# Two low-part tiles moved by 128 bytes, and six small vector loads moved up the load queue, in a decoder trunk on one core

## The chip, the cores and the metric

The kernel runs on one core of a Trainium2 chip. The metric is the device time of one execution in microseconds (us). TensorE (PE) multiplies, and loads the stationary operand of a product in an instruction of its own (PEld); VectorE (DVE) and ScalarE (ACT) work element by element; SyncE (SP) issues all the loads here.

## The reference

Two layers, each of three sublayers on a stream `x` of 256 tokens by 1024 channels in float32:

```python
x = layer_norm(ALPHA * x + 0.5 * swiglu(x, ffn_w1[l, 0], ffn_w2[l, 0]), ...)
x = layer_norm(ALPHA * x + hybrid_mixer(x, w_in[l], ...), ...)
x = layer_norm(ALPHA * x + 0.5 * swiglu(x, ffn_w1[l, 1], ffn_w2[l, 1]), ...)
```

`swiglu` multiplies by 1024x5632 weights, gates (`silu(g) * u`) and multiplies by 2816x1024. `hybrid_mixer` has one 1024x7168 input projection (parts b, c, v, x, y and two merge gates), a short gated convolution, a linear recurrence with 256x256 gate matrices per head, two 1024x1024 output projections (`w_out_conv`, `w_out_rnn`), a gated merge, and a last 1024x1024 projection `w_o`.

## The kernel before

**Split products.** Every operand of a product is split in a high part and a low part (`hi` and `lo` for weights, `xh` and `xl` for the stream, `yh` and `yl` or slots for other activations), and a product is three matmuls: high by high, low activation by high weight, high activation by low weight. `high` (L202) makes the high part of a weight unit on ACT, `low` (L207) the low part on DVE.

**Weight units.** Weights come in units of 1 MB (128 partitions by 2048 floats), numbered in the order of use. SP loads a unit into `raw` (four buffers, L198), then ACT and DVE fill `hi` and `lo` (six buffers each). The main loop emits up to `LOOK` = 6 units ahead of the units that are used up. Units 0 and 1 are loaded in pieces ahead of it, between the loads of `x`.

**Shapes.** In the first part of each sublayer the weights are stationary (128x128) and the stream moves, 256 columns at a time: these are the groups `gu`, `c`, `v`, `b`, `x`, `y`, `ga`, `gb`, `wc`, `wr`, `rg`, all recorded at `mm` (L216). `mm_cols` issues eight products of `xh` by `hi`, eight of `xl` by `hi` and eight of `xh` by `lo`, then takes the next 128 weight columns (`wr` and `rg` in shorter groups). In `form_b` (group `acc`) and in `filler` (group `fill`) it is the other way round: activations are stationary and weights move, 512 columns at a time (256 in a few). `filler` opens each sublayer, while the second half of the tokens is still being normalised; it ends in products of the shape that follows it.

**Addresses.** The tiles of the pool `const` lie one behind the other in the order of their lines, then come the buffers of `raw`, `hi`, `lo` and the activation slots, all of whose sizes are multiples of 4096 bytes in a partition. `xh` and `xl` have 8192 bytes in a partition, `yh` and `yl` (eight rows of 256 floats and a spare of 128 floats) 8704, `gB` and `bB` 4096 each, `vec` 832, `hbm` and `hrg` 128 each, `sp2` and each of the six `sp_` tiles 64; `tiny` and `mhalf` take 32 each. From `xh` to the first weight buffer that makes 43584 = 85 x 512 + 64 bytes. So modulo 512 bytes the weights, and the activation slots, lie 64 past `xh`, and `xl`, `yh` and `yl` lie level with `xh`. `split` (L231) places the hidden rows of `swiglu` 16 floats (64 bytes) into `yh` and `yl`, which puts those level with the weights.

**The opening.** The steps of the first sublayer are `opening` (units 0 and 1, with transposes of `x` among the products), then the products of units 2 and 3 in `fill`, then `gu` from unit 4 on. `load_vectors` issues six small loads into the tile `rows` (L129): biases, convolution taps and recurrence parameters, 104 KB in all. `vectors_pe` turns them on PE (group `vps`, L135), ACT copies the result to `vec`, and `vectors_post` works out a few constants on DVE. They are first used in the mixer. The scheduler keeps each engine's queue in order once it is laid down: PE runs its instructions in program order.

Of the kernel before, what the change touches and what calls it, by code (L numbers as in the profile page):

```python
# [9 lines left out]
F32 = mybir.dt.float32  # L10
# [4 lines left out]
P = 128  # L15
# [25 lines left out]
def trunk_kernel(  # L41
# [21 lines left out]
    _, S, D = x.shape  # L63
    DEPTH = w_in.shape[0]
    DFF = ffn_w2.shape[2]
    NT = S // P
    KD = D // P
# [5 lines left out]
    NPAIR = KD // 2  # L73

    const = ctx.enter_context(tc.tile_pool(name="const", bufs=1))
# [7 lines left out]
    def slot(name, dt=F32):  # L83
        return act.tile([P, 2, S], dt, tag="s", name=name)

    def bank(name):
        return pw.tile([P, 512], F32, tag="w", name=name)

    def f(ap):
        return ap.bitcast(F32)  # L90

    ident = const.tile([P, P], F32, name="ident")
    xtok = const.tile([P, NT, D], F32, name="xtok")
    xh = const.tile([P, KD, S], F32R, name="xh")
    xl = const.tile([P, KD, S], F32R, name="xl")
    yh = const.tile([P, KD * S + 128], F32R, name="yh")
    yl = const.tile([P, KD * S + 128], F32R, name="yl")
    gB = const.tile([P, D], F32, name="gB")
    bB = const.tile([P, D], F32, name="bB")
# [2 lines left out]
    NV = 13 * KD  # L102
    O_BM, O_SC, O_RC, O_RB, O_RG, O_A = 0, 2 * KD, 5 * KD, 9 * KD, 10 * KD, 12 * KD
    vec = const.tile([P, DEPTH, NV], F32, name="vec")
    hbm = const.tile([P, DEPTH, 2 * KD], F32, name="hbm")
    hrg = const.tile([P, DEPTH, 2 * KD], F32, name="hrg")
    sp2 = const.tile([P, DEPTH, KD], F32, name="sp2")
    tiny = const.tile([P, 1], F32, name="tiny")

# [9 lines left out]
    def load_vectors():  # L119
        r = slot("rows")[:NV, :, :P]  # L120
        for src, o, n in (
            (b_merge, O_BM, 2 * KD),
            (sc_w.rearrange("l k d -> l (k d)"), O_SC, 3 * KD),
            (rc_w.rearrange("l k d -> l (k d)"), O_RC, 4 * KD),
            (rc_b, O_RB, KD),
            (rg_b.rearrange("l k d -> l (k d)"), O_RG, 2 * KD),
            (a_param, O_A, KD),
        ):
            nc.sync.dma_start(out=r[o : o + n], in_=src.rearrange("l (r p) -> r l p", p=P))  # L129
        rows.extend(r[:, l, :] for l in range(DEPTH))  # L130
# [7 lines left out]
    def vectors_post():  # L138
        nc.vector.tensor_scalar_mul(hbm, vec[:, :, O_BM : O_BM + 2 * KD], 0.5)
        nc.vector.tensor_scalar_mul(hrg, vec[:, :, O_RG : O_RG + 2 * KD], 0.5)  # L140

        a = vec[:, :, O_A : O_A + KD]
        shp = [P, DEPTH, KD]
        t = {n: const.tile(shp, F32, name=f"sp_{n}") for n in ("na", "e", "base", "d", "q", "acc")}
        nc.vector.scalar_tensor_tensor(t["na"], a, -1.0, a, op0=ALU.mult, op1=ALU.min)
        nc.gpsimd.memset(t["base"], math.e)
        nc.gpsimd.tensor_tensor(t["e"], t["base"], t["na"], op=ALU.pow)
        nc.vector.tensor_scalar_add(t["d"], t["e"], 2.0)
        nc.vector.reciprocal(t["d"], t["d"])
        nc.vector.tensor_mul(t["d"], t["d"], t["e"])  # L150
        nc.vector.tensor_mul(t["q"], t["d"], t["d"])
        nc.vector.tensor_scalar_mul(t["acc"], t["q"], 1.0 / 19)
        for n in (17, 15, 13, 11, 9, 7, 5, 3):
            nc.vector.scalar_tensor_tensor(
                t["acc"], t["acc"], 1.0 / n, t["q"], op0=ALU.add, op1=ALU.mult
            )
        nc.vector.scalar_tensor_tensor(t["acc"], t["acc"], 1.0, t["d"], op0=ALU.add, op1=ALU.mult)
        nc.vector.tensor_scalar(t["na"], a, -1.0, 0.0, op0=ALU.mult, op1=ALU.max)
        nc.vector.scalar_tensor_tensor(
            t["na"], t["acc"], 2.0, t["na"], op0=ALU.mult, op1=ALU.add  # L160
        )
        nc.vector.tensor_scalar_mul(sp2, t["na"], 2.0)


    units = []
# [13 lines left out]
    def unit_half(parts, h):  # L179

        n = 512 // len(parts)
        srcs = []
        for i, (w, c0) in enumerate(parts):
            s = w[h * 512 : (h + 1) * 512, c0 : c0 + n].rearrange("(k p) c -> p k c", p=P)
            srcs.append((i * n, s))
        return unit(srcs, (4, 512))

    def load_unit(u, parts=1):
        u.raw = praw.tile([P, 2048], F32, tag="raw", name="raw")
        u.hi = phi.tile([P, 2048], F32R, tag="hi", name="hi")  # L190
        u.lo = plo.tile([P, 2048], F32R, tag="lo", name="lo")
        view = lambda t: t.rearrange("p (a b) -> p a b", b=u.shape[-1])
        u.h, u.l = view(u.hi), view(u.lo)
        n = u.shape[0] // parts
        for i in range(parts):
            ks = slice(i * n, (i + 1) * n)
            for c0, src in u.srcs:
                u.load = nc.sync.dma_start(out=view(u.raw)[:, ks, c0 : c0 + src.shape[-1]], in_=src[:, ks])  # L198
# [29 lines left out]
    def row(t, k, n, shift=0):  # L228
        return t[:, shift + k * S : shift + (k + n) * S]

    def split(name, v, j=NPAIR, shift=0):  # L231


        if j < NPAIR:
            h, lo = (row(t, 2 * j, 2, shift).rearrange("p (a b) -> p a b", b=S) for t in (yh, yl))
        else:
            h, lo = slot(name + "h", F32R), slot(name + "l", F32R)
        nc.scalar.copy(h, v)
        nc.vector.tensor_sub(lo, v, f(h))
        return h, lo  # L240
# [163 lines left out]
    def ffn(l, i, n, last):  # L404
        w1, w2 = ffn_w1[l, i], ffn_w2[l, i]
        hs = {}
        opens = (l, i) == (0, 0)
        nfill = NFILL if opens else 1
        fill = [unit_half([(w1, 256 * b), (w1, DFF + 256 * b)], h) for b in range(nfill) for h in range(2)]
        ga, up = {}, {}  # L410
        for j in range(nfill, NPF):
            ga[j] = unit_a(w1, 256 * j)
            up[j] = unit_a(w1, DFF + 256 * j)
        us = [unit_b(w2, q) for q in range(NPF)]

        def swish(g, u, shape, name):

            v = slot(name)
            o = v.rearrange("p a b -> p (a b)")[:, : shape]
            nc.scalar.activation(o, g, AF.Tanh, scale=0.5)  # L420
            nc.vector.scalar_tensor_tensor(o, o, 1.0, g, op0=ALU.add, op1=ALU.mult)
            nc.vector.tensor_mul(o, o, u)  # L422
            return v

        tok = {}

        def post_fill(t, b, ps):
            tok[t, b] = swish(ps[:, 0:256], ps[:, 256:512], 256, "hf")

        filler(fill, post_fill, not opens)  # L430

        def fill_transposes(b):
            ps = bank("hT")
            h, lo = slot("h0h", F32R), slot("h0l", F32R)
            for t in range(NT):
                v = tok[t, b].rearrange("p a b -> p (a b)")
                for c in range(2):
                    with tc.issue_after(last_mm[0]):
                        nc.tensor.transpose(
                            ps[:, c * S + t * P : c * S + (t + 1) * P], v[:, c * P : (c + 1) * P], ident  # L440
                        )
            p3 = ps.rearrange("p (c s) -> p c s", s=S)
            nc.scalar.copy(h, p3)
            nc.vector.tensor_sub(lo, p3, f(h))
            hs[b] = h, lo

        banks = {}

        def pe(j, which, u):
            b = bank("gu")  # L450
            banks[j, which] = b
            for c in range(2):
                mm_cols(b[:, c * S : (c + 1) * S], u, c * P, x_pairs())

        def post(j):
            v = swish(banks[j, 0], banks[j, 1], 512, "hv")
            hs[j] = split("h", v, j - 5 if 5 <= j < 9 else NPAIR, 16)

        for j in range(nfill, NPF):
            step(lambda j=j: pe(j, 0, ga[j]), None, 1, [ga[j]])  # L460
            if 1 <= j - nfill <= nfill:
                step(lambda b=j - nfill - 1: fill_transposes(b))
            step(lambda j=j: pe(j, 1, up[j]), lambda j=j: post(j), 1, [up[j]])

        form_b(us, lambda q, kk, t: [v[:, kk, t * P : (t + 1) * P] for v in hs[q]], 0.25, l, n, last)
# [216 lines left out]
    for hh in range(2):  # L682
        load_x(hh)
        load_unit(units[hh], 2)
    done, freed = 2, 0
    for i, (pe, post, free, need) in enumerate(steps):
        while i and done < min(len(units), freed + LOOK):
            emit_unit(units[done])
            done += 1
            if done == 4:  # L690
                load_vectors()
        if pe:
            pe()
        if post:
            post()
        freed += free
        if i == 2:
            vectors_pe()
            vectors_post()
# [29 lines left out]
```

## Time and profile before

| | us |
|---|---|
| three runs | 1213.77, 1220.48, 1223.33 |
| median | 1220.48 |
| the profiled execution | 1221.89 |
| its span | 1220.1 |

PE is busy for 99% of the span (DVE for 67%, ACT for 48%). Products are pipelined, so the time that one takes from start to end is longer than the distance between starts; what counts is the distance, which the chain of waits gives as the length of a piece divided by its count. A row of the chain has the start of the piece in us from the start of the span, its length in us, and what ran. A row of the timeline has start, length (to the modelled end of the last product), engine, line, operation, what it writes and reads, shape and count. A row of the stretches has the bounds, the length, the busy time and count on PE, PEld, DVE, ACT and POOL, the granted TensorE clock, the share of time in which DMA engines were busy, and GB/s.

### The profile page before, as it was taken

Reading aid. Unit: us, or ns where it says so; the run is one execution under the profiler, and the core shown is the slowest. Engines: PE = TensorE matmul, PEld = TensorE weight load, DVE = VectorE, ACT = ScalarE, POOL = GpSimd, SP = SyncE. Lnnn points to the kernel's source line nnn. Section 1 sums busy time; section 2 is a strip of 40 time slices with the busy share of each in tenths; the row PEclk is TensorE's granted clock in tenths of the full one; section 3 lists DMA queues with packets and bytes.
Section 4 is the critical chain, followed back from the end, with each engine's and each line's share of the span. In section 5 each row is a group of like instructions: output and inputs, shape, how many; then the busy total and the mean of one; then the engine's idle time right before and its main releaser. Section 6 shows DMA issues by size and latency. Waiting matters only on the chain.

```text
span 1220.1 us, 20487 instructions
## 1 busy us (share of the span) xinstructions
PE 1209.1 (99%) x8995; PEld 1143.6 (94%) x8995; DVE 821.1 (67%) x786; ACT 590.9 (48%) x566; POOL 14.9 (1%) x20
## 2 busy tenths in 40 slices
PE   8999999999999999999999999999999999999997
PEld 6999888999999899998899998899999998999986
DVE  5856447968997686654585654587689966856533
ACT  5544434774675354443354443366745744544420
POOL 0000000000000000000000000000000000000000
PEclk9999999999999999999999999999999999999999
DMA  9966553756576475655476665474755753856510
GB/s 309 305 200 225 194 186 115 244 194 208 176 238 208 139 229 189 239 189 191 138 237 190 230 200 180 138 237 145 230 183 173 242 173 104 276 181 234 196 47 35
DMA packets 186133, 236.31 MB, mean 194 GB/s; under 512 B 4076, under 2 KB 168124, under 8 KB 186044
## 3 DMA queue, kind: packets, MB, share of 16 engines
q1 hardware_dynamic: 186044, 235.00, 58.5%
q8 instruction: 70, 1.15, 0.4%
q14 instruction: 19, 0.16, 0.0%
HBM read 233.94 MB, written 1.05 MB: 193 GB/s over the span
## 4 chain that ended last, share of the span: by engine, by line
PE 97%; DMA 2%; DVE 0%; SPq 0%; ACT 0%; issue 0%; DVEq 0%; ACTq 0%
PE gu L216 35%; PE acc L216 23%; PE fill L216 5%; PE b L216 4%; PE ga L216 4%; PE wr L216 4%; PE gb L216 4%; PE y L216 4%; PE wc L216 4%; PE c L216 4%; PE v L216 4%; PE x L216 2%; PE rg L216 2%; DMA raw<-in_ffn_w_dram 1%; PE xT L262 1%; DMA rows<-in_rg_b_dram 0%
## 5 line engine op out<-in xcount | busy, mean ns | idle before, releaser
L207 DVE TENSOR_TENSOR lo<-raw,hi 128x2048 fp32r<-128x2048 f32 (+1 forms) x218 | 493.4, 2269 | 234.6 <-ACT hi L202 234.2
L202 ACT CAST hi<-raw 128x2048 fp32r<-128x2048 f32 (+1 forms) x217 | 411.1, 1901 | 461.2 <-issue 170.3
L216 PE MATMUL gu<-xh,hi 128*128 128x256 f32 x1248 | 167.6, 277 | 0.0
L216 PE MATMUL gu<-xl,hi 128*128 128x256 f32 x1248 | 167.0, 276 | 0.0
L216 PE MATMUL gu<-xh,lo 128*128 128x256 f32 x1248 | 167.0, 276 | 0.0
L216 PEld LDWEIGHTS gu<-xh,hi 128*128 128x128 f32 x1248 | 153.7, 188 | 0.3
L216 PEld LDWEIGHTS gu<-xh,lo 128*128 128x128 f32 x1248 | 153.3, 188 | 0.0
L216 PEld LDWEIGHTS gu<-xl,hi 128*128 128x128 f32 x1248 | 153.3, 188 | 0.0
L216 PE MATMUL acc<-hi,hl 128*128 128x512 f32 (+1 forms) x196 | 73.8, 376 | 0.0
L216 PE MATMUL acc<-hi,hh 128*128 128x512 f32 (+1 forms) x196 | 73.7, 376 | 0.0
L216 PE MATMUL acc<-lo,hh 128*128 128x512 f32 (+1 forms) x196 | 73.7, 376 | 0.0
L422 DVE TENSOR_TENSOR hv<-hv,gu 128x512 f32<-128x512 f32 x39 | 26.8, 687 | 51.7 <-PE gu L216 51.6
L216 PE MATMUL acc<-hi,yh 128*128 128x512 f32 (+1 forms) x136 | 51.5, 379 | 0.0
L216 PE MATMUL acc<-hi,yl 128*128 128x512 f32 (+1 forms) x136 | 51.3, 377 | 0.0
L216 PE MATMUL acc<-lo,yh 128*128 128x512 f32 (+1 forms) x136 | 51.2, 377 | 0.0
L266 ACT CAST xh<-xT 128x512 fp32r<-128x512 f32 x24 | 13.5, 588 | 75.0 <-PE xT L262 74.7
L288 DVE SCALAR_TENSOR_TENSOR xtok<-acc,xtok 128x512 f32<-128x512 f32 (+1 forms) x25 | 16.7, 668 | 46.6 <-PE acc L216 46.3
L216 PEld LDWEIGHTS acc<-hi,hl 128*128 128x128 f32 x196 | 36.9, 188 | 6.8
L216 PEld LDWEIGHTS acc<-hi,hh 128*128 128x128 f32 x196 | 36.9, 188 | 6.7
L216 PEld LDWEIGHTS acc<-lo,hh 128*128 128x128 f32 x196 | 36.9, 188 | 6.7
L216 PE MATMUL fill<-hi,xh 128*128 128x512 f32 x112 | 31.2, 401 | 0.5 <-DVE hi L202 0.5
L216 PE MATMUL fill<-hi,xl 128*128 128x512 f32 x112 | 31.1, 400 | 0.0
(181 smaller groups left out, 1842.3 us busy)
## 6 DMA issues: line engine op xcount, KB each, us to landing
raw<-in_ffn_w_dram SPq DMA_DIRECT2D x122, 1024.0 KB, 5.1
raw<-in_w_in_dram SPq DMA_DIRECT2D x56, 1024.0 KB, 5.1
raw<-in_ffn_w_dram SPq DMA_DIRECT2D x16, 512.0 KB, 4.9
raw<-in_w_out_conv_dram SPq DMA_DIRECT2D x8, 1024.0 KB, 5.8
raw<-in_w_out_rnn_dram SPq DMA_DIRECT2D x8, 1024.0 KB, 5.4
raw<-in_w_o_dram SPq DMA_DIRECT2D x8, 1024.0 KB, 4.9
raw<-in_rg_w_dram SPq DMA_DIRECT2D x4, 1024.0 KB, 5.5
gB<-in_ln_g_dram SPq DMA_DIRECT2D x6, 512.0 KB, 6.4
```

What stands on the lines that cost most here:

```text
L202: (copy or nc.scalar.copy)(u.hi[:, part], u.raw[:, part])
L207: nc.vector.tensor_sub(u.lo[:, part], u.raw[:, part], f(u.hi[:, part]))
L216: last_mm[0] = nc.tensor.matmul(ps, lhs, rhs, start=first, stop=last).ins
L262: nc.tensor.transpose(ps[:, i * P : (i + 1) * P], xtok[:, t, c * P : (c + 1) * P], ident)
L266: nc.scalar.copy(dh, v)
L288: nc.vector.scalar_tensor_tensor(zc, ps, c, zc, op0=ALU.mult, op1=ALU.add)
L422: nc.vector.tensor_mul(o, o, u)
```

## The change

Tiles of `const` that were allocated late, or inside `vectors_post`, are now allocated between the large ones. `hbm` (128 bytes) lies between `xh` and `xl`, the six `sp_` tiles (384 bytes) between `xl` and `yh`, `hrg` (128 bytes) between `yh` and `yl`. The sum of sizes ahead of the weights stays as it was. Modulo 512 bytes `xl` and `yl` thus lie 128 past `xh` and `yh`, and 64 past the weights, where they were 64 ahead of them; `xh` and `yh` lie where they lay. The hidden rows of `swiglu` start 64 bytes into `yh` and 448 bytes into `yl`, and so stay level with the weights. The six vector loads are issued behind the loads of unit 1, no longer behind those of the first units of the loop.

```diff
     xh = const.tile([P, KD, S], F32R, name="xh")
+    hbm = const.tile([P, DEPTH, 2 * KD], F32, name="hbm")
     xl = const.tile([P, KD, S], F32R, name="xl")
+    sp = {n: const.tile([P, DEPTH, KD], F32, name=f"sp_{n}") for n in ("na", "e", "base", "d", "q", "acc")}
     yh = const.tile([P, KD * S + 128], F32R, name="yh")
+    hrg = const.tile([P, DEPTH, 2 * KD], F32, name="hrg")
     yl = const.tile([P, KD * S + 128], F32R, name="yl")
...
-    hbm = const.tile([P, DEPTH, 2 * KD], F32, name="hbm")
-    hrg = const.tile([P, DEPTH, 2 * KD], F32, name="hrg")
...
-        shp = [P, DEPTH, KD]
-        t = {n: const.tile(shp, F32, name=f"sp_{n}") for n in ("na", "e", "base", "d", "q", "acc")}
+        t = sp
...
-    def split(name, v, j=NPAIR, shift=0):
+    def split(name, v, j=NPAIR, shift=(0, 0)):
...
-            h, lo = (row(t, 2 * j, 2, shift).rearrange("p (a b) -> p a b", b=S) for t in (yh, yl))
+            h, lo = (row(t, 2 * j, 2, n).rearrange("p (a b) -> p a b", b=S) for t, n in zip((yh, yl), shift))
...
-            hs[j] = split("h", v, j - 5 if 5 <= j < 9 else NPAIR, 16)
+            hs[j] = split("h", v, j - 5 if 5 <= j < 9 else NPAIR, (16, 112))
...
     for hh in range(2):
         load_x(hh)
         load_unit(units[hh], 2)
+    with tc.issue_after(units[1].load.ins):
+        load_vectors()
     done, freed = 2, 0
...
             done += 1
-            if done == 4:
-                load_vectors()
```

The order of instructions moves in two places. The first is SP's queue near the start of the program. `raw_110` is unit 1 before and `raw_116` after; `raw_227`, `raw_234`, `raw_248`, `raw_254`, `raw_260` are units 2 to 6 before, and `raw_240`, `raw_247` units 2 and 3 after; `rows` is the tile of the vectors. In brackets stand the semaphores that SP waits for; the eight of DMAHW go round, so a load waits for the landing of one issued eight or so before it. Before:

```order
L198 DMA raw_110<-in_ffn_w1_dram 128x2x256 [waits DMAHW3_49]
L198 DMA raw_227<-in_ffn_w1_dram 128x4x256 [waits DMAHW4_49]
L198 DMA raw_227<-in_ffn_w1_dram 128x4x256 [waits DMAHW5_49]
L198 DMA raw_234<-in_ffn_w1_dram 128x4x256 [waits DMAHW6_49]
L198 DMA raw_234<-in_ffn_w1_dram 128x4x256 [waits DMAHW7_49]
L198 DMA raw_248<-in_ffn_w1_dram 128x8x256 [waits DMAHW0_49,DVE_49]
L198 DMA raw_254<-in_ffn_w1_dram 128x8x256 [waits DMAHW2_49,DMAHW3_49,DMAHW1_49,DVE_49]
L198 DMA raw_260<-in_ffn_w1_dram 128x8x256 [waits DMAHW5_49,DMAHW4_49,DVE_49]
L129 DMA rows_241<-in_b_merge_dram 16x2x128
L129 DMA rows_241<-in_sc_w_dram 24x2x128
```

The same place of SP's queue after the change:

```order
L198 DMA raw_116<-in_ffn_w1_dram 128x2x256 [waits DMAHW3_49]
L130 DMA rows_123<-in_b_merge_dram 16x2x128 [waits DMAHW4_49]
L130 DMA rows_123<-in_sc_w_dram 24x2x128 [waits DMAHW5_49]
L130 DMA rows_123<-in_rc_w_dram 32x2x128 [waits DMAHW6_49]
L130 DMA rows_123<-in_rc_b_dram 8x2x128 [waits DMAHW7_49]
L130 DMA rows_123<-in_rg_b_dram 16x2x128 [waits DMAHW0_49]
L130 DMA rows_123<-in_a_param_dram 8x2x128 [waits DMAHW1_49]
L198 DMA raw_240<-in_ffn_w1_dram 128x4x256 [waits DMAHW2_49]
L198 DMA raw_240<-in_ffn_w1_dram 128x4x256 [waits DMAHW3_49]
L198 DMA raw_247<-in_ffn_w1_dram 128x4x256 [waits DMAHW4_49]
```

The six loads have moved from behind units 4 to 6 to ahead of unit 2, and unit 2's two halves now wait for the landing of the third and the fourth piece of unit 1.

The second place is PE's queue, in the `fill` products of units 2 and 3 ahead of the first `gu`. Here `hi_228` and `lo_229` are unit 2, `hi_235` and `lo_236` unit 3; `fill_272` and `fill_285` are the two token halves. Before:

```order
L216 MATMUL fill_285<-lo_229,xh_78 128x512 x4
L216 MATMUL fill_272<-hi_235,xh_78 128x512 x4
L216 MATMUL fill_272<-hi_235,xl_79 128x512 x4
L216 MATMUL fill_272<-lo_236,xh_78 128x512 x3
L135 MATMUL vps_298<-ident_76,rows_241 128x104 x2
L216 MATMUL fill_272<-lo_236,xh_78 128x512
L216 MATMUL fill_285<-hi_235,xh_78 128x512 x4
```

After, with `lo_242` for unit 2 and `hi_248`, `lo_249` for unit 3:

```order
L216 MATMUL fill_291<-lo_242,xh_78 128x512 x4
L136 MATMUL vps_304<-ident_76,rows_123 128x104 x2
L216 MATMUL fill_278<-hi_248,xh_78 128x512 x4
L216 MATMUL fill_278<-hi_248,xl_80 128x512 x4
L216 MATMUL fill_278<-lo_249,xh_78 128x512 x4
L216 MATMUL fill_291<-hi_248,xh_78 128x512 x4
```

The two transposes of the vectors stand eleven products earlier on PE, between unit 2 and unit 3. On ACT the scaling of `xtok` (L401) moves ahead of the high part of unit 3, and on DVE the constants of `vectors_post` are spread among the low parts of later units.

## The prediction

> **What bounds the kernel now.** I read the page first, for the busy times.
>
> ```profile
> PE 1209.1 (99%) x8995; PEld 1143.6 (94%) x8995; DVE 821.1 (67%) x786; ACT 590.9 (48%) x566; POOL 14.9 (1%) x20
> ```
>
> PE is never short of work for long, so the time can fall in two ways only: less idle or slow-clocked time on PE, or products that follow each other at a shorter distance. For that distance I read the chain of waits in order of time (start, length, what).
>
> ```profile
> 200.69 6.43 PE fill L216 x28
> ...
> 218.91 10.91 PE x L216 x96
> ...
> 344.06 21.76 PE y L216 x192
> ...
> 403.90 17.69 PE acc L216 x78
> ...
> 438.83 16.35 PE gu L216 x144
> ...
> 815.25 11.31 PE x L216 x96
> ...
> 945.27 22.61 PE y L216 x192
> ...
> 1007.46 17.72 PE acc L216 x78
> ...
> 1042.42 16.96 PE gu L216 x144
> 1059.38 0.44 PE hT L439 x4
> ```
>
> The same 192 products of `y` take 21.76 us in layer one and 22.61 us in layer two: 113.3 and 117.8 ns apart, 4.4 ns of difference. Call these the short and the long beat. The long beat runs unbroken from 815.25 to 1007.46, and again from 1042.42 to 1059.38, and stops at four transposes. The same products of layer one, from 218.91 to 403.90, took 184.99 us against 192.21: 7.2 us. The `gu` piece adds 16.96 - 16.35 = 0.6. So this execution lost 7.8 us to the long beat. It isn't the clock or more traffic, as the view of the two stretches shows.
>
> ```profile
> 219.00:403.80 184.80, 184.80 (x1633) 184.80 (x1632) 153.18 (x157) 115.75 (x142) 0.00 (x0) 1.00 0.63 205
> 815.25:1007.40 192.15, 192.15 (x1633) 192.15 (x1633) 154.11 (x158) 116.06 (x142) 0.00 (x0) 1.00 0.61 197
> ```
>
> Clock 1.00 in both, DMA share and the other engines alike. Without the long beat the profiled execution would have taken 1221.89 - 7.8 = 1214.1, which is where the fastest of the three runs lies (1213.77). I take the spread of the three, 9.6 us, for different shares of long beat; the median then carries about 6.4.
>
> The other loss is in the opening, in the timeline.
>
> ```profile
> 17.17 1.91 ACT L202 CAST hi<-raw 128x2048 fp32r<-128x2048 f32 x1 [1.65 <-DMA raw<-in_ffn_w_dram]
> 19.12 2.29 DVE L207 TENSOR_TENSOR lo<-raw,hi 128x2048 fp32r<-128x2048 f32 x1 [2.14 <-ACT hi L202]
> 20.25 1.08 PE L216 MATMUL fill<-hi,xh 128*128 128x512 f32 x4
> 22.08 1.08 PE L216 MATMUL fill<-lo,xh 128*128 128x512 f32 x4
> 22.99 1.08 PE L216 MATMUL fill<-hi,xh 128*128 128x512 f32 x4
> 25.74 1.08 PE L216 MATMUL fill<-hi,xh 128*128 128x512 f32 x4
> 27.57 0.85 PE L216 MATMUL fill<-lo,xh 128*128 128x512 f32 x3
> 30.32 0.37 PE L135 MATMUL vps<-ident,rows 104*128 104x104 f32 x2 [1.90 <-DMA rows<-in_rg_b_dram]
> 30.84 1.91 PE L216 MATMUL fill<-hi,xh 128*128 128x512 f32 x4
> 35.12 1.07 PE L216 MATMUL gu<-xh,hi 128*128 128x256 f32 x8
> 36.03 1.07 PE L216 MATMUL gu<-xl,hi 128*128 128x256 f32 x8
> ```
>
> PE stops for the vectors until 30.32, and the twelve products from 30.84 to 35.12 take 4.28 us where twelve like them, from 22.99 to 25.74, took 2.75. The stretches name the reason: the idle 1.8 us is followed by 3.4 us at half clock.
>
> ```profile
> 28.50:30.30 1.80, 0.00 (x0) 0.01 (x1) 1.55 (x2) 1.64 (x2) 0.00 (x0) 1.00 1.08 348
> 30.70:34.10 3.40, 3.40 (x9) 2.62 (x9) 3.40 (x6) 2.73 (x4) 0.00 (x0) 0.50 1.03 338
> ```
>
> **The vectors.** Undisturbed, the group of 27.57 would end its four products 2.75 / 3 = 0.92 later, at 28.49, and twelve more would bring `gu` to 31.24. It came at 35.12: 3.9 us late. The two transposes themselves stay, some 0.3 of it, so up to 3.6 us can be had. After the change they stand where the products of 25.74 begin. The loads are issued right behind unit 1's.
>
> ```profile
> 9.05 8.05 DMA raw<-in_ffn_w_dram
> 24.47 5.60 DMA rows<-in_rg_b_dram
> ...
> raw<-in_ffn_w_dram SPq DMA_DIRECT2D x16, 512.0 KB, 4.9
> ```
>
> Unit 2's last byte landed at 9.05 + 8.05 = 17.10. Its 1 MB at 348 GB/s takes 3.0 us, so unit 1 had landed by 14.1, and its third piece (256 KB, 0.75 us) by 13.35. The last vector load now waits for unit 1's second piece, near 12.6; with 5.6 us to landing it is there by 18.2, seven us ahead of need. Queued behind it on SP are all units from 2 on. Unit 2's first half leaves at 13.4 instead of earlier than 9.05, the second at 14.1. Lower bound of the delay: the 104 KB of the vectors at 348 GB/s, 0.3 us. Upper bound: 4.9 us from issue to landing, 14.1 + 4.9 = 19.0, 1.9 late, though those 4.9 hold other loads ahead in the queue. Unit 2's high part was ready at 19.08 for a product at 20.25, its low part at 21.41 for one at 22.08: slack 1.2 and 0.7 us. So PE stalls by 0 to 1.2 us; I take 0.3, since the queue is nearly drained by then and the first row of unit 2 pays little but the gap. Unit 3 follows 3 us behind for products at 25.74 and 27.57, and the 1.9 us scaling now ahead of it on ACT fits in that. Unit 4 is wanted at 31.5 and landed near 23; the constants on DVE are 0.17 us pieces. Opening: **-3.3 us** (-2.4 to -3.6).
>
> [...]
>
> **The addresses.** What changes is the distance, modulo 512 bytes, between the stream that moves and the weights that are loaded meanwhile. Before it is -64 in every 256-column group. After, it is -64 in products with `xh` or `yh` and +64 in those with `xl` or `yl`. In `acc` it is 0 and stays 0; in `fill` (weights move) it was +64 and becomes -64 for `xl`. The chain holds that such distances may matter: 512-column products at distance 0 run 17.69 / 78 = 226.8 ns apart, those at +64 run 6.43 / 28 = 229.6. Against that speaks that the shapes' stationary operands differ too.
>
> [...]
>
> There are 7200 such products: 3744 `gu`, eight groups of 384, 192 each of `x` and `rg`. The distance now steps twice in 24 products, four times in `wr`'s and in `rg`'s 64 times in all: 312 + 224 + 16 + 64 + 64 = 680 steps. In the trace a beat is chosen where the sequence is disturbed and then kept for hundreds of products: the long one came after transposes and after `fill`, and left at transposes. A step of distance every eight products, if it is a disturbance, should end a long stretch within a few products. What does a step cost while the beat is short? Lower bound: at 35.12, `fill` gives way to `gu` and the first eight products take 0.91, as any eight at 113.3 ns. Upper bound, a dearer entry in the timeline:
>
> ```profile
> 803.27 1.09 PE L216 MATMUL c<-xh,hi 128*128 128x256 f32 x8
> 804.20 1.07 PE L216 MATMUL c<-xl,hi 128*128 128x256 f32 x8
> ```
>
> These eight take 0.93 for 0.907, 23 ns. Shape and distance both change there; in a step the shape stays, so I take a value near the lower row, 3 ns: 680 x 3 = 2.0 us (0 to 15.6). Long beat: **-7.8**; steps: **+2.0**. In `fill` at best 112 products with `xl` gain 2.8 ns, 0.3 us, taken at nothing. The constants moved between the tiles are written and read by the same instructions as before.
>
> Sum against the profiled execution: 1221.89 - 3.3 - 7.8 + 2.0 = **1212.8 us**. With the long beat gone, most of what set that execution 1.4 above the median is gone too, so I take it for the median.
>
> **The rivals.**
> - *128 bytes change nothing in the beat* (distances -64 and +64 act alike, or none acts). Only the opening gains: median 1220.48 - 3.3 = 1217.2, and between 1213.77 - 3.3 = 1210.5 and 1223.33 - 3.3 = 1220.0 by the share of long beat. For it: `fill` and `acc` alone show a distance at work. Against it: nothing in these rows. [...]
> - *Every step costs a re-entry*: the 23 ns of 803.27, times 680, is 15.6 us; 1221.89 - 3.3 - 7.8 + 15.6 = 1226.4, slower than before. It decides from (3.3 + 7.8) / 680 = 16 ns a step. Much the same comes if products at +64 keep the long beat, as `fill` at +64 keeps its longer distance throughout: 2400 products with `xl` or `yl` times 4.4 ns is 10.6, and a re-entry of up to 23 ns behind each of some 340 gives up to 7.8: 1221 to 1229.
> - *The long beat everywhere*: 7200 x 4.4 = 31.7; 1221.89 - 3.3 - 7.8 + 31.7 = 1242.5. Only if no short stretch survives a step.
> - *Faster than the short beat*: products at +64 nearer to the 110 ns that the four transposes of 1059.38 show (0.44 / 4); 2400 x 3.3 = 7.9 less than the forecast: 1204.9. Transposes have half the columns, so this is far-fetched.
>
> **How the numbers follow.** Forecast 0.40 (its own range 1210 to 1216), no effect 0.30, dear steps or a long beat at +64 0.20, long beat everywhere 0.05, faster than short 0.05. The range 1208 to 1228 leaves out the last two and the upper end of the third, and part of nothing else. A measurement of this kernel can tell about 1%, 12 us, from no change. Faster by over 1% means below 1208.3: the last case and a little of the forecast, 0.08. Slower by over 1% means above 1232.7: the long beat everywhere and some of the dear steps, 0.08. The rest, 0.84, is within 1%.
>
> **What would show it.** Right: no row of PE waiting for `rows`, clock 1.00 from 28 us on, `gu` beginning near 31.8; in the chain every 192 products in 21.8 to 21.9 us in both layers, no piece at 22.6. The first rival shows a whole mixer or `swiglu` at 22.6 again and others at 21.76. Dear steps show in the timeline as eights of 0.93 where the distance changes; a long beat at +64 as eights of 0.94 with `xl` beside 0.91 with `xh`. I am wrong on the opening if unit 2's first product waits for more than an us, or the half clock comes anyway.

## The result, and the profile after

The changed kernel took 1242.84 us (median of four runs, 1242.51 to 1243.19). The kernel before, run beside it, took 1221.9 (four runs, 1213.77 to 1223.77). The ratio is 1.0158, with a 95% interval of 1.0117 to 1.0199: slower by 1.6%. The forecast was 1212.8 and the range ended at 1228. The four runs lie within 0.7 us of each other; before they spread over 10 us.

The profiled execution took 1242.79 us, with a span of 1241.0. The page still shows PE busy throughout, with the same number of instructions and 23 us more of busy time:

```profile
PE 1232.0 (99%) x8995; PEld 1165.9 (94%) x8995; DVE 820.9 (66%) x786; ACT 590.1 (48%) x566; POOL 14.9 (1%) x20
```

The chain of waits (start, length, what) answers to the pieces shown in the prediction:

```profile
32.43 16.96 PE gu L216 x144
...
61.56 73.48 PE gu L216 x624
...
201.68 6.47 PE fill L216 x28
...
220.31 11.30 PE x L216 x96
...
350.33 22.61 PE y L216 x192
...
389.91 22.40 PE wr L216 x192
...
464.71 96.09 PE gu L216 x816
...
962.67 22.61 PE y L216 x192
```

All but one of the long pieces are on the long beat, in both mixers and all four `swiglu`: 22.61 / 192 = 117.8 ns, 96.09 / 816 = 117.8. The exception is `wr`, with 22.40 / 192 = 116.7. Before, `y` took 21.76 in layer one, and the 624 products that are 73.48 here took 70.75. The mixer's stretch of layer one has the clock at full speed, and the same DMA share as the two stretches of before:

```profile
220.40:412.20 191.80, 191.80 (x1633) 191.80 (x1632) 153.28 (x156) 115.33 (x142) 0.00 (x0) 1.00 0.60 196
```

Where the 20.9 us between the two profiled executions lie, group by group in the two chains: -2.85 in the opening (the first `gu` at 32.27 for 35.12), +3.75, +4.2, +4.2 and +3.6 in the four `swiglu`, +7.4 in the mixer of layer one, +0.1 in that of layer two (which was long before too), and about +0.5 in `fill` and `acc`.

The timeline after shows the opening as it was meant to be, but for one wait:

```profile
20.32 1.21 PE L216 MATMUL fill<-hi,xh 128*128 128x512 f32 x4
...
22.65 1.20 PE L216 MATMUL fill<-lo,xh 128*128 128x512 f32 x4 [0.18 <-DVE lo L207]
...
26.48 0.34 PE L136 MATMUL vps<-ident,rows 104*128 104x104 f32 x2
...
32.27 1.10 PE L216 MATMUL gu<-xh,hi 128*128 128x256 f32 x8
```

PE no longer waits for the vectors (`vps` has no wait ahead of it), and the stretches that held the wait and the half clock are busy at clock 1.00:

```profile
28.00:30.00 2.00, 2.00 (x11) 1.60 (x10) 2.00 (x1) 1.69 (x1) 0.00 (x0) 1.00 1.09 349
30.00:32.00 2.00, 2.00 (x10) 1.64 (x9) 1.91 (x2) 0.57 (x3) 0.00 (x0) 1.00 1.09 349
```

The first product with unit 2's low part waits for that part (22.65). It starts 2.33 us after the unit's first product (20.32), where before the two lay 1.83 apart (20.25 and 22.08): unit 2's later landing costs 0.5 us.

How the long beat comes about can be read where the same piece starts. Before, and then after, right behind four transposes:

```profile
51.81 1.17 PE L216 MATMUL gu<-xh,hi 128*128 128x256 f32 x8
52.81 1.07 PE L216 MATMUL gu<-xl,hi 128*128 128x256 f32 x8
53.72 1.07 PE L216 MATMUL gu<-xh,lo 128*128 128x256 f32 x8
```

```profile
49.59 1.17 PE L216 MATMUL gu<-xh,hi 128*128 128x256 f32 x8
50.59 1.10 PE L216 MATMUL gu<-xl,hi 128*128 128x256 f32 x8
51.54 1.10 PE L216 MATMUL gu<-xh,lo 128*128 128x256 f32 x8
52.48 0.40 PE L216 MATMUL gu<-xh,hi 128*128 128x256 f32 x2
```

The first eight take 1.00 us in both. Of the next eight, with `xl`, before needs 0.91 and after 0.95; and the third eight, with `xh` again, whose addresses the change leaves alone, stay at 0.94. Product by product, in the starts of single products of the trace, 11 of the 15 places where 256-column products begin look like this after the change: within three to seven products the gap comes down to 113 ns (207, 118, 114, 113, 113, ...), the first product with the low part takes 118 to 119, and those behind it 117.8 on average, those with the high part too. At the other four places the first eight don't get short at all. Only `wr`, whose groups are of six and of two products, leaves the long beat again: behind six products with `yl` the gaps of the next six, with `yh`, come down (117, 115, 115, 113, 113, 114), and the next product with `yl` ends that too (119). Before, 13 of the 15 places came down to 113 and stayed there to the end of the stretch.

### The profile page after: what moved, and what is told of

It reads as the page before. It is cut to its first block, busy times and chain, and to the rows that moved or that the text cites. A ratio compares the mean times of both kernels' runs of the same rounds, so it can differ in the third digit from the quotient of the medians.

```text
span 1241.0 us, 20489 instructions
## 1 busy us (share of the span) xinstructions
PE 1232.0 (99%) x8995; PEld 1165.9 (94%) x8995; DVE 820.9 (66%) x786; ACT 590.1 (48%) x566; POOL 14.9 (1%) x20
## 4 chain that ended last, share of the span: by engine, by line
PE 98%; DMA 1%; DVE 0%; ACT 0%; SPq 0%; issue 0%; DVEq 0%; ACTq 0%
PE gu L216 36%; PE acc L216 23%; PE fill L216 5%; PE c L216 4%; PE b L216 4%; PE y L216 4%; PE gb L216 4%; PE ga L216 4%; PE wc L216 4%; PE v L216 4%; PE wr L216 4%; PE rg L216 2%; PE x L216 2%; DMA raw<-in_ffn_w_dram 1%; PE xT L262 1%; DVE lo L207 0%
## 5 line engine op out<-in xcount | busy, mean ns | idle before, releaser
L216 PE MATMUL gu<-xh,hi 128*128 128x256 f32 x1248 | 172.8, 281 | 0.0
L216 PE MATMUL gu<-xl,hi 128*128 128x256 f32 x1248 | 172.6, 280 | 0.0
L216 PE MATMUL gu<-xh,lo 128*128 128x256 f32 x1248 | 171.9, 280 | 0.0
L216 PEld LDWEIGHTS gu<-xh,hi 128*128 128x128 f32 x1248 | 158.3, 189 | 0.3
L216 PEld LDWEIGHTS gu<-xl,hi 128*128 128x128 f32 x1248 | 158.2, 188 | 0.0
L216 PEld LDWEIGHTS gu<-xh,lo 128*128 128x128 f32 x1248 | 157.6, 188 | 0.0
L216 PE MATMUL acc<-hi,hl 128*128 128x512 f32 (+1 forms) x196 | 73.7, 376 | 0.0
L216 PE MATMUL acc<-hi,hh 128*128 128x512 f32 (+1 forms) x196 | 73.7, 376 | 0.0
L216 PE MATMUL acc<-lo,hh 128*128 128x512 f32 (+1 forms) x196 | 73.7, 376 | 0.0
L216 PE MATMUL acc<-hi,yh 128*128 128x512 f32 (+1 forms) x136 | 51.5, 379 | 0.0
L216 PE MATMUL acc<-hi,yl 128*128 128x512 f32 (+1 forms) x136 | 51.3, 377 | 0.0
L216 PE MATMUL acc<-lo,yh 128*128 128x512 f32 (+1 forms) x136 | 51.2, 377 | 0.0
L216 PEld LDWEIGHTS acc<-lo,hh 128*128 128x128 f32 x196 | 36.9, 188 | 6.8
L216 PEld LDWEIGHTS acc<-hi,hl 128*128 128x128 f32 x196 | 36.9, 188 | 6.7
L216 PEld LDWEIGHTS acc<-hi,hh 128*128 128x128 f32 x196 | 36.9, 188 | 6.7
L216 PE MATMUL fill<-lo,xh 128*128 128x512 f32 x112 | 30.9, 398 | 0.2 <-DVE lo L207 0.2
L216 PE MATMUL fill<-hi,xh 128*128 128x512 f32 x112 | 30.6, 395 | 0.2 <-DVE hi L202 0.2
```

The lines of the kernel that those rows point to most:

```text
L216: last_mm[0] = nc.tensor.matmul(ps, lhs, rhs, start=first, stop=last).ins
```

## The experiments

Two theories stood at the start. A: the *distance* +64 between the moving operand and the weights itself brings the long beat. B: the *alternation* brings it, each step of distance being a disturbance. Whether the opening gained what the prediction said was a third question. All kernels but `e9_y_only_old_order` and `e10_addresses` issue the vector loads as the change does. Addresses were moved as the change moves them, by the order of the small tiles in `const` and the shifts of the hidden rows in `split`, with `acc` left at distance 0. Six lines were added above `mm`, so that L222 is here what L216 was, and L142 what L136 was. Distances are those of the prediction, modulo 512 bytes.

**Vector loads alone.** The addresses are those of before.

```diff
+    with tc.issue_after(units[1].load.ins):
+        load_vectors()
...
-            if done == 4:
-                load_vectors()
```

> Only the six vector loads move; every tile keeps its place of before. The opening should give what it gave in the whole change: gu begins near 32.3 us instead of 35.1, no half clock. If the long beat of the whole change comes from the addresses, short and long beats should be mixed as before: 1211 to 1221 us. If it comes from the order of the opening, the long beat is everywhere here too: about 1243 us.

Measured: 1225.76 us (median of ten, 1211.93 to 1230.11) beside 1220.51 (19 runs, 1211.96 to 1228.64); ratio 1.0025 [0.9984, 1.0065]. The chain of its profiled run, 1230.11 us:

```profile
60.96 73.50 PE gu L222 x624
...
349.33 22.61 PE y L222 x192
...
463.24 92.49 PE gu L222 x816
```

Both beats, as before, in other places: the vector loads alone don't bring the long beat everywhere, and the run with the addresses alone, below, shows that these bring the 20 us. The median lies above the expected 1211 to 1221. The opening alone can't be told from no change, since the mixture of beats moves the time by 18 us from run to run. One place may have been made worse: the piece of 624 `gu` is long here and in the other four profiles that have the vector loads moved and `gu` at -64 (73.5 us), and short in the two with the loads in their old place (70.75). Seven profiles suggest that the order of the opening bears on the beat that begins there; they don't show it.

**Only the tiles of `yl` moved.** `xl` at -64, `yl` at +64; the step comes in `rg`, `wc` and `wr` alone, and both theories are asked what the mixer does behind its first `rg`. `hrg` and the `sp_` tiles go behind `yl`.

```diff
-    hbm = const.tile([P, DEPTH, 2 * KD], F32, name="hbm")
     xl = const.tile([P, KD, S], F32R, name="xl")
...
     yh = const.tile([P, KD * S + 128], F32R, name="yh")
-    hrg = const.tile([P, DEPTH, 2 * KD], F32, name="hrg")
+    hbm = const.tile([P, DEPTH, 2 * KD], F32, name="hbm")
     yl = const.tile([P, KD * S + 128], F32R, name="yl")
```

> Vector loads moved as in the whole change; of the tiles only yl moves by 128 bytes, so the distance alternates in rg, wc and wr alone and stays -64 elsewhere. If a step of distance by itself brings the long beat and the beat is then kept, the swiglu parts are mixed as before and the mixer is long from its first rg on (192 products in 22.6 us in wc, ga, y and wr). If only products at +64 are long, rg, wc and wr hold eights of 0.94 with yl beside 0.91 with yh, and c, v, b, ga, y, gb can be short (21.8). About 1211 to 1229 us.

Measured: 1225.52 us (eight runs, 1224.1 to 1229.0); ratio 1.0046 [1.0024, 1.0067]. It told nothing apart: both mixers were on the long beat from their first product of `x` on, ahead of the first `rg`. It was made again below with the vector loads in their old place.

**No alternation: everything at +64.** `hbm` goes ahead of `xh`, the other small tiles behind `yl`.

```diff
-    xh = const.tile([P, KD, S], F32R, name="xh")
     hbm = const.tile([P, DEPTH, 2 * KD], F32, name="hbm")
+    xh = const.tile([P, KD, S], F32R, name="xh")
...
-            hs[j] = split("h", v, j - 5 if 5 <= j < 9 else NPAIR, (16, 112))
+            hs[j] = split("h", v, j - 5 if 5 <= j < 9 else NPAIR, (112, 112))
```

> Vector loads moved; xh, xl, yh and yl all lie 128 bytes further on, so the distance is +64 in every 256-column group and never alternates; in fill it is -64 throughout. If alternation is the cause, beats are mixed as before or all short: 1211 to 1221 us. If the distance +64 is the cause, all products are long: 1243 us or more, and fill at -64 may lose its three-step pattern.

Measured: 1240.22 us (four runs, 1235.72 to 1243.59); ratio 1.017 [1.0126, 1.0213]. The chain:

```profile
201.64 6.54 PE fill L222 x28
...
465.10 96.11 PE gu L222 x816
...
1078.08 92.49 PE gu L222 x816
```

The long beat needs no alternation: 14 of the 15 places took it and kept it (96.11 / 816 = 117.8). One piece, the last (92.49 / 816 = 113.3), was short from its second product on and stayed so for all 816. So +64 by itself did not end that short stretch; a stretch at +64 began short at one place of 15. `fill`, whose distance becomes -64, loses: 6.54 for 6.43.

**No alternation: everything level.** `sp2` (64 bytes) goes ahead of `xh`, and the shifts become (0, 0).

```diff
+    sp2 = const.tile([P, DEPTH, KD], F32, name="sp2")
     xh = const.tile([P, KD, S], F32R, name="xh")
...
+            hs[j] = split("h", v, j - 5 if 5 <= j < 9 else NPAIR, (0, 0))
```

> Vector loads moved; all four tiles lie level with the weights modulo 512 bytes, distance 0 everywhere, fill included, as acc has it already. If distance 0 is what keeps acc at 226.7 ns, fill falls to 226.7 (1 us in all) and the 256-column products stay at the short beat throughout: 1210 us in every run. If the beat depends only on where a stretch is entered, it is mixed: 1211 to 1221. If the distance doesn't matter outside acc, fill stays at 229.6.

Measured: 1258.08 us (four runs, 1257.79 to 1258.47); ratio 1.0319 [1.0275, 1.0363], the slowest of all. The chain:

```profile
203.26 6.38 PE fill L222 x28
...
354.48 23.04 PE y L222 x192
```

23.04 / 192 = 120.0 ns for every 256-column product, a third beat. `fill`, whose distance becomes 0 too, gains: 6.38 for 6.43 and 6.47. Of all the distances tried, the one at which `fill` is fastest (6.38 against 6.42 to 6.55 in the other profiles) is the slowest for the 256-column products.

**Alternation by 256 bytes.** Distances -64 and +192. By B this is as bad as the change; if the distance counts modulo 256 bytes, +192 is -64 and nothing happens.

```diff
     xh = const.tile([P, KD, S], F32R, name="xh")
     hbm = const.tile([P, DEPTH, 2 * KD], F32, name="hbm")
+    hrg = const.tile([P, DEPTH, 2 * KD], F32, name="hrg")
     xl = const.tile([P, KD, S], F32R, name="xl")
...
+            hs[j] = split("h", v, j - 5 if 5 <= j < 9 else NPAIR, (16, 80))
```

> Vector loads moved; xl and yl lie 256 bytes further on than xh and yh instead of 128, so the distance alternates between -64 and +192. If a step of distance as such throws a stretch out of the short beat, every stretch turns long at the ninth product, as in the whole change: 1243 us. If what counts is the distance modulo 256 bytes, -64 and +192 are the same and short and long are mixed as with the vector loads alone: 1212 to 1230 us, with stretches that keep the short beat across the steps.

Measured: 1225.28 us (eight runs, 1214.73 to 1229.19) beside 1226.94; ratio 0.9977 [0.994, 1.0014]. The chain:

```profile
218.18 10.91 PE x L222 x96
...
343.33 21.76 PE y L222 x192
...
944.54 22.61 PE y L222 x192
```

The mixer of layer one holds the short beat through all its steps, in `y` as in `x`, and that of layer two is long: the mixture of before. So for this pair the distance counts modulo 256 bytes: -64 and +192 acted alike, and going from one to the other is then no step at all. Whether a step of 128 bytes, as in the change, is a disturbance, this run can't tell.

**Three other distances**, the same for all tiles: +128 (`hbm` and `sp2` ahead of `xh`, shifts of 96), -96 (shifts of 24) and -32 (`tiny` ahead, shifts of 8). They ask whether further from level is better.

```diff
+    sp2 = const.tile([P, DEPTH, KD], F32, name="sp2")
     hbm = const.tile([P, DEPTH, 2 * KD], F32, name="hbm")
+    xh = const.tile([P, KD, S], F32R, name="xh")
...
+            hs[j] = split("h", v, j - 5 if 5 <= j < 9 else NPAIR, (96, 96))
```

> Vector loads moved; distance +128 in every 256-column group and in fill, no alternation. So far -64 gives short or long, +64 nearly always long, 0 a third beat of 120.0 ns. If the cost falls with the distance from level (a collision of the two streams), +128 holds the short beat throughout: 1209 to 1213 us. If only -64 is good, it is as +64 or 0: 1240 to 1258 us.

> Vector loads moved; distance -96 everywhere. On the side of -64 away from level: if being further from level makes the short beat surer, short in nearly all stretches: 1209 to 1215 us. If -64 is a narrow optimum: 1225 to 1258 us.

> Vector loads moved; distance -32 everywhere, half way from -64 to level. If the beat worsens step by step towards level: long throughout or the 120.0 ns of level, 1243 to 1258 us. If the beat goes by 64-byte blocks, as -64 (mixed, 1212 to 1230 us).

Rows of `y` in the chains, in this order:

```profile
352.72 22.78 PE y L222 x192
```

```profile
349.35 22.53 PE y L222 x192
...
964.95 22.78 PE y L222 x192
```

```profile
351.81 22.72 PE y L222 x192
```

| distance | us (runs) | ratio | beats of 256-column products, ns |
|---|---|---|---|
| -64, before | 1220.51 (19) | 1 | 113.3 or 117.8 |
| -64 and +192 | 1225.28 (8) | 0.9977 [0.994, 1.0014] | 113.3 or 117.8 |
| -64 and +64, the change | 1242.84 (4) | 1.0158 [1.0117, 1.0199] | 117.8 |
| +64 | 1240.22 (4) | 1.017 [1.0126, 1.0213] | 117.8, once 113.3 |
| -96 | 1248.0 (2) | 1.0181 [1.0127, 1.0236] | 117.3 or 118.7 |
| -32 | 1248.08 (2) | 1.0182 [1.0134, 1.023] | 118.3 |
| +128 | 1250.6 (2) | 1.0203 [1.0154, 1.0251] | 118.7 or 120.0 |
| 0 | 1258.08 (4) | 1.0319 [1.0275, 1.0363] | 120.0 |

The ratios are to the kernel before as it ran beside each: 1221.9 us for the change, 1220.51 for +64 and 0, 1226.94 for the others (nine runs). The idea that further from level is better fell: +128 is the furthest, and next to the worst. Of the distances tried only -64 reaches 113.3 ns often.

**`yl` alone, once more, with the vector loads where they were before.** The tiles are those of the second experiment.

```diff
-    with tc.issue_after(units[1].load.ins):
-        load_vectors()
...
+            if done == 4:
+                load_vectors()
```

> The vector loads stay where they were, xh, xl and yh too; only yl moves by 128 bytes (+64 in yl products of rg, wc and wr). With this opening the mixer of layer one began short in the profile of before. Theory now: the first group at +64 throws a short stretch into the long beat, and the long beat then keeps itself at -64 too. Then a mixer that enters short is short until its first rg and long from there to its end, in c, v, b, ga, y and gb as well, where every distance is -64 (48 products in 5.65 us, not 5.44). Rival: only products at +64 are long; then c, v, b, ga, y and gb stay short (192 in 21.76) and wc and wr lie between.

Measured, one run: 1225.2 us beside 1219.87 (19 runs, 1212.22 to 1223.51). This time both mixers began on the short beat. The chain:

```profile
216.94 10.91 PE x L222 x96
227.85 2.82 PE rg L222 x24
230.66 5.65 PE c L222 x48
...
346.56 22.61 PE y L222 x192
...
819.79 10.91 PE x L222 x96
830.70 2.85 PE rg L222 x24
833.55 5.65 PE c L222 x48
```

`x` runs at 10.91 / 96 = 113.6 ns; `rg`, the first group with `yl`, at 117.5; and `c`, which has neither `yh` nor `yl` in it and lies at -64 throughout, stays at 5.65 / 48 = 117.7, as does all behind it up to `y`. The timeline shows the moment:

```profile
227.69 0.39 PE L222 MATMUL rg<-yh,hi 128*128 128x256 f32 x2
227.91 0.40 PE L222 MATMUL rg<-yl,hi 128*128 128x256 f32 x2
228.15 0.40 PE L222 MATMUL rg<-yh,lo 128*128 128x256 f32 x2
228.38 0.40 PE L222 MATMUL rg<-yh,hi 128*128 128x256 f32 x2
```

Two products at -64 take 0.22 us, the first two at +64 take 0.24, and the next two, at -64 again, 0.23. In the starts of single products the first with `yl` takes 119 ns, and of those behind it in `rg` none is below 115. In that run all `gu`, whose tiles are at -64, were short. In the profiles of before, of -64 with +192 and of the first order of groups below, the mixer that began short kept 113.3 ns through its `rg` groups. So here the first product at +64 behind products at -64 ended the short stretch, and the long beat then kept itself up at -64.

That takes something from both theories. In the change, in the run with its addresses alone (below) and here, 25 stretches came down to 113 ns before they met a product at +64, and all 25 ended at the first one. Yet the stretch that was short at +64 from its start, in the third experiment, stayed short for 816 products. What ends a short stretch is thus, as far as that one stretch goes, the step to +64 and not +64 itself (B, for steps of 128 bytes and one way only); and where there is no step, +64 lets a stretch begin long at 14 places of 15 (A).

**The addresses of the change alone**, with the vector loads where they were before (the diff is the one just shown, on the changed kernel).

> Only the addresses of the whole change; the vector loads stay where they were. As the whole change is long nearly everywhere in every run, the difference to it is the opening alone, free of the mixture of beats: 1242.8 + 2.9 = 1245.7 us if the opening gives what the shift of gu shows, with PE waiting 1.9 us for the vectors and half clock behind it; 1242.8 if the opening's gain is lost again later.

Measured: 1243.62 us (four runs, 1243.45 to 1243.95); ratio 1.0197 [1.015, 1.0243]. The expected 1245.7 counted on a half clock that this run's profile doesn't have. With the beat fixed at 117.8 the kernel repeats itself to 0.5 us, so the vector loads' place can be priced here, though from runs of two occasions: 1243.62 - 1242.84 = 0.8 us. The profiles agree: in the chain the first `gu` stands at 33.32 for 32.43.

```profile
33.32 16.95 PE gu L222 x144
```

The timeline and a stretch of this run, and after them the same of the run with `yl` alone, which has the old order as well:

```profile
29.90 0.37 PE L142 MATMUL vps<-ident,rows 104*128 104x104 f32 x2 [1.31 <-DMA rows<-in_rg_b_dram]
...
30.00:32.00 2.00, 2.00 (x11) 1.63 (x12) 1.62 (x2) 1.46 (x3) 0.00 (x0) 1.00 1.03 322
```

```profile
29.91 0.37 PE L142 MATMUL vps<-ident,rows 104*128 104x104 f32 x2 [1.95 <-DMA rows<-in_rg_b_dram]
...
30.00:32.00 2.00, 2.00 (x11) 1.66 (x12) 1.35 (x2) 1.47 (x3) 0.00 (x0) 1.00 0.99 325
```

PE waits for the vectors, 1.31 and 1.95 us for the 1.90 of before, and yet the clock stays at 1.00. Of three profiles with the old order, one (before's) has the half clock.

**Can the short beat be had on purpose?** Two orders of the mixer's groups, with before's addresses and the moved vector loads. `x0` and `x1` are the two groups of transposes. In the first order they follow each other ahead of `v`, in the second both stand behind it. The second has an effect that was not foreseen: the first `rg` has to wait for its activations, and PE stops once more inside the mixer.

```diff
-        "c0 x0 v0 x1 x2 x3 rg0 c1 rg1 b0 v1 rg2 b1 rg3 sqrt c2 v2 b2 c3 v3 b3 lru0 gb0 lru1 "
+        "c0 x0 x1 v0 x2 x3 rg0 c1 rg1 b0 v1 rg2 b1 rg3 sqrt c2 v2 b2 c3 v3 b3 lru0 gb0 lru1 "
```

```diff
+        "c0 v0 x0 x1 x2 x3 rg0 c1 rg1 b0 v1 rg2 b1 rg3 sqrt c2 v2 b2 c3 v3 b3 lru0 gb0 lru1 "
```

> Vector loads moved, distances -64 as before; in the mixer the two groups of x transposes follow each other (c0 x0 x1 v0 ...), so that the 256-column products are interrupted once instead of twice. In the runs so far the long beat of a mixer began at the products behind the second group. If the second interruption is what brings it, mixers are mostly short: 1210 to 1218 us. If any last interruption does it as often, the same mixture as with the vector loads alone: median near 1225.

> As the run with one interruption, but both groups of x transposes stand behind v0, right ahead of the x products, where the long beat began so far (c0 v0 x0 x1 x2 ...). If what matters is the interruption's place, long mixers as often as with the vector loads alone, median near 1225; if the single interruption is what helps, 1210 to 1218.

The first: 1224.34 us (ten runs, 1219.83 to 1229.43), ratio 1.0055 [1.0025, 1.0085]; in its profile one mixer was long, the other short. A single interruption by transposes thus doesn't bring the hoped-for 1210 to 1218. The second: 1216.9 us (ten runs, 1215.55 to 1225.04), ratio 0.9993 [0.9965, 1.0021]. The second's timeline in layer two, and `y` in its chain:

```profile
826.55 1.10 PE L222 MATMUL x<-xl,hi 128*128 128x256 f32 x8
827.50 1.10 PE L222 MATMUL x<-xh,lo 128*128 128x256 f32 x8
830.21 0.74 PE L222 MATMUL rg<-yh,hi 128*128 128x256 f32 x4 [1.61 <-ACT yh L244]
830.79 1.07 PE L222 MATMUL c<-xh,hi 128*128 128x256 f32 x8
831.70 1.07 PE L222 MATMUL c<-xl,hi 128*128 128x256 f32 x8
...
944.74 21.76 PE y L222 x192
```

The mixer was entered long (eight products in 0.95); after a stop of 827.50 + 0.94 to 830.21, 1.8 us, it runs short (0.91) to its end. Each mixer thus pays 1.8 us for a second draw and may save up to 7.2. It was the fastest of the versions with moved vector loads, 7.4 us below the first order on the same occasion (three of its ten runs lie above that one's fastest), but is the same as before within the interval. Nothing here forces the short beat; a stop seems to offer a new draw, which came out short in both mixers of the one profile.

## Why the prediction was wrong

- **What bounds the kernel, and the two beats: right.** The time is PE's distance between products, at a clock of 1.00. The size was nearly right too: for *the long beat everywhere* the prediction had 1242.5, and it came out at 1242.84, some of that by luck. Between the two profiled executions the beats cost 23.3 where the rival had 23.9, the opening gave 2.85 where it had 3.3, and 0.5 in `fill` and `acc` was not foreseen. That rival had a chance of 0.05.
- **The step that failed:** "A step of distance every eight products, if it is a disturbance, should end a long stretch within a few products." In the groups of eight they ended none: after the change the long beat runs through hundreds of such steps (`y` in 22.61 us, 117.8 ns, in both layers). Only in `wr` did they end some (116.7 ns). The steps work the other way: the first product at +64 ended every *short* stretch that met one, 25 of 25, and the long beat, once there, kept itself up at -64. I had the trace's own evidence that a beat is kept for hundreds of products, and used it only for leaving the long beat, not for falling into it. Eight products at +64 in every 24 decided nearly the whole (`y` at 117.8 ns in both layers).
- **Long beat -7.8 and steps +2.0:** in their place +23.3, the four `swiglu` (15.8) and the mixers (7.5). The sum missed by 29 us there. The price of 3 ns for a step came from two entries where the shape changed, and those said nothing about a distance that is kept.
- **The rival on dear steps** came near the mechanism ("products at +64 keep the long beat") but let the products with `xh` come back to the short beat for at most 23 ns each time. The eights with `xh` behind an eight with `xl` did not (51.54: 0.94); only the sixes of `wr` did.
- **The opening, -3.3: wrong in size.** It gives 0.8. The wait for the vectors went, as said. Of the 2.5 us that are missing, 1.7 (the 3.6 that the prediction said could be had, less the wait of 1.90) went with the half clock of one profiled execution, which two further profiles with a wait don't have. Another 0.6 was the wait itself, 1.31 us in the run that gives the 0.8 and 1.90 before, and unit 2's later landing cost 0.5 where I had 0.3. The clock was 0.50 behind before's wait of 1.90 us, and 1.00 behind those of 1.95 and 1.31. My reading, that such a wait suffices, holds in one of the two profiles that have one of 1.9 us or more; what else decides the clock, no run shows.
- **`fill`:** expected 0 to -0.3 us; 28 products took 6.47 for 6.43, no gain. The assumption that `fill` is better at -64 than at +64 was wrong: with -64 throughout they take 6.54.
- **"128 bytes change nothing in the beat"**, the first rival (0.30), fell: with one order of loads, the same products and a mean clock of 0.998 to 0.999 in every run, the time was 1225.76 us at -64, 1240.22 at +64 and 1258.08 at 0, by address alone. By what way the address acts, no run shows.
- **A slip ahead of the prediction:** the activation slots are 2048 bytes long, not a multiple of 4096. They are multiples of 512, so the distances stand.

## What to carry to other kernels

When PE is the bound (here busy for 99% of the span) and products follow each other at full clock, look at the distance between products of the same shape in several places. Here one shape had two values, 113.3 and 117.8 ns, and each was a state that lasted for up to 1632 products; so an edit must be judged by what it lets the state fall into: one product in three, at +64, was enough to hold nearly all at 117.8. Price a stall that a single profile shows only after a second profile has it too, the clock above all: the half clock stood in one profile of the three with the old order. Where a kernel's runs spread over 10 us, compare single effects on a version whose state is fixed: there 0.8 us could be read.

## What the runs showed of the hardware

- The distance between a 256-column product of these 4-byte operands and the next, each with a weight load, went in these runs with the address of the moving operand relative to the weights: 113.3 or 117.8 ns at -64 and, alternating with it, at +192 (256 bytes on), 117.8 and once 113.3 at +64, 117.3 or 118.7 at -96, 118.3 at -32, 118.7 or 120.0 at +128, 120.0 at 0. In 1242 us of kernel that is worth up to 46 us (1258.08 against the 1211.93 of the fastest run). The 512-column products of `fill` followed another order: 28 took 6.38 us at distance 0, 6.43 at +64 and 6.54 at -64.
- At four of the distances (-64, +64, -96, +128) two beats are seen. Both were kept for 1632 products at -64, the short one for 816 at +64. A step from -64 to +64 ended every short stretch that came to one (25 of 25); in the profile of -64 with +192, the mixer that began short kept 113.3 ns through all its steps. The long beat ended at four transposes (before, 1059.38) and at a stop of 1.8 us (the second order of groups, 827.50 + 0.94 to 830.21); whether the beat is drawn anew at such a place is open.
- Open: whether the distance to the weights counts or the address of the stream's tiles alone, since the weights stood at the same addresses in every run; why 113.3 ns came often at -64 alone, what decides which beat a stretch begins on, and by what way the address acts.
